# Gate of 1536 columns by Strassen units, the last 512 by token blocks, the embedding product ahead of the GLU

## The chip, the cores and the metric

The kernel runs on one core of one Trainium2 chip. The metric is the device time of one execution in microseconds; three runs of the kernel before took 1724.1, 1725.99 and 1729.99, median 1725.99. A core has five engines with a queue each: TensorE (PE, matmuls into PSUM), VectorE (DVE), ScalarE (ACT), GpSimd (POOL) and SyncE (SP, which here only issues transfers). Each works through its own instructions in order and waits for the others by semaphores. Transfers between DRAM and the on-chip memory SBUF are done by 16 DMA engines. In this kernel DVE and ACT read matmul results from PSUM; POOL and the transfers work on SBUF.

## The reference

Sequence 1024 (tokens), model width D = 2048, everything float32. Cut to what matters:

```python
hn = rmsnorm(h, norm_gain)
proj = hn @ w_in                     # 2048 x 4096: pool input | pool gate | ssm input | ssm gate
ya = pool_mixer(pool_in, w_pool, pool_scale) * silu(pool_gate)   # trailing means, windows 2/4/8/16
g  = gelu(ssm(ssm_in))               # state space, groups of 16 channels
hg = g @ w_glu                       # 1024 x 2048
yb = hg[:, :1024] * sigmoid(hg[:, 1024:]) * silu(ssm_gate)
h  = h + concat([ya, yb]) @ w_out    # 2048 x 2048
h  = h + (p @ w_ple) * sigmoid(h @ w_ple_gate)   # 256 x 2048 and 2048 x 2048: embedding and gate
out = rmsnorm(h, final_gain)
```

## The kernel before

Most data is kept transposed: channels on the 128 partitions, tokens along the rows, in two halves of HT = 512 tokens. A float32 product is made of three matmuls of a rounded type: both operands are split into a high and a low part (ACT casts the high part, DVE subtracts to get the low one), and high x high, high x low and low x high are added up in PSUM. One matmul has 128 x 128 fixed and 128 x 512 moving operands. All splits of weights (`split`, buffer `w`) and of data (`slot`, tag S, 32 buffers) are instructions of ACT and DVE that PE waits for.

The program is a list of steps of about 12 matmuls, written in order. `emit(s)` issues, for step s: the loads of weight chunks that have a free buffer (`raw`, three), the stores that are due (`store` keeps each one or more steps back), the splits of the weights of up to four steps ahead as far as six `w` buffers allow (a Strassen step takes two, so three steps), then the functions hung on the step ahead of it ("pre"), a slice of the background work (state space, pooling windows), the step's matmuls, and the functions behind it ("post"). So the order on every engine is the order of these calls, and a pre function that waits on ACT or DVE holds back the weight splits behind it. Tiles of 128 x 512 come from one rotating pool (`st`, 11 buffers): a new tile waits until the one eleven allocations back has been left by all its users, a transfer included. SP's transfers use eight completion semaphores in turn, so one waits until the eighth before it has landed.

The stages, with their place in the profile: input product (0 to 815 us) with the state-space work and the pooling windows beside it; the GLU (819 to 988), the output product (988 to 1296), and the gate with the embedding product (1296 to the end).

GLU and output product are made by `unit`: one of Strassen's seven-product schemes over quadrants. A unit takes 1024 input channels and two blocks of 256 output columns for all tokens, and has seven products (PRODS) of two steps, 12 matmuls a step, 168 in all, where a direct product has 192. The weights' sums are made on DVE (`sums`, four of 128 x 1024 a unit), the sums of the data beforehand and once for all units of a slab (`sums_load`, `sums_make`, stored in `cm_d`), and the 28 combinations of a slab are loaded and split two a step (`comb_load`, `comb_split`, tile `cb`). The products' parts are put together by a post function: `glu_post`, `o_post`. In the output product a slab n is one half of the 2048 input channels; `xt_load` brings the residual (from `xT_d`, in slab 1 from `h_d`), each part is added to it by DVE (tile `xtl`), and the sum is stored to `h_d`.

The gate runs per half h and group cg of 512 output columns in `wide_step`s: tokens on the partitions, the data as fixed operand, the weights (128 x 512) as moving one, 16 steps, then `embed`, two steps of the embedding product into other banks. `sig` takes the sigmoid, `join` multiplies by the embedding product and adds to `nat`, the token-major copy of h, which POOL's `hs_pre` (high plus low part), PE's `back` (transposes, tile `bk`) and `back_copy` make. `squares` sums squares and lets POOL multiply by the gain. In the last group (cg 3, h 1) the split weights stay (`wl`) and the work goes by blocks of 128 tokens, the last of them in two halves of 256 columns (`last_part`), so that little is left behind the last matmul.

The input product's last two blocks, 2 and 3, have their second half of tokens last (from `i_last0` to `i_last1`); then the GLU's first unit follows, then the pooling product of group 1 (`pool_mm(1)`), then the other units. POOL makes `lw` and the add in `lm` for the state space (`ss_l`) and the adds of the pooling windows (`pool_win`, tile `pf`).

## Time and profile before

| | us |
|---|---|
| median of three runs | 1725.99 |
| the profiled execution | 1725.38 |
| its span on the core | 1723.6 |
| PE busy | 1682.1 |
| DVE busy | 1108.0 |
| ACT busy | 660.3 |
| POOL busy | 282.4 |

The profile names an instruction by its line, its engine and the tiles it writes and reads, as `mm<-hn,w`: it writes a bank named mm and reads hn and w. L99 is the helper `tt` (an operation on two tensors), so its rows tell DVE's and POOL's work apart by tiles. A row of a group has the count, the busy time in all, the mean of one in ns, and the idle time of the engine ahead of it with what ended it. The chain of waits goes back from the last instruction, at each step to what released it. A row by stretches has the stretch, its length, then busy time and count of PE, PE's weight loads, DVE, ACT and POOL, PE's granted clock, the DMA engines' busy share and GB/s. A transfer row has the count, the size of one, and the median time from issue to landing.

### The profile page before, as it was taken

To read this page: it belongs to the slowest core of one execution; us is meant where nothing else is said; L and a number is where in the kernel's file an instruction comes from. 1 tells how busy PE (TensorE), PEld (TensorE's weight loads), DVE (VectorE), ACT (ScalarE), POOL (GpSimd) and SP (SyncE) were. 2 spreads that over 40 slices of the span, in tenths; PEclk is the share of its full clock that TensorE was granted. 3 is DMA by queue.
4 is the path that set the end of the run, shared out by engine and by line. 5 is a ranking of instruction groups with operands and counts; after the bars stand their busy time and mean duration, and the time that the engine had idled before them with its cause. 6 is when DMAs were issued, how large, how long until landed. Compare 5 with 4: busy or idle time off the path is not lost.

```text
span 1723.6 us, 22772 instructions
## 1 busy us (share of the span) xinstructions
PE 1682.1 (98%) x7766; PEld 1390.3 (81%) x7766; DVE 1108.0 (64%) x1992; ACT 660.3 (38%) x1379; POOL 282.4 (16%) x327
## 2 busy tenths in 40 slices
PE   8999999999999999999899999999999999999997
PEld 7788877888888888787688778888888777877786
DVE  5763688468786655555967887695574655466642
ACT  6651255352114542333533532252232433343432
POOL 0057135000000214311100000000000332023320
PEclk9999999999999999999999999999999999999999
DMA  8863434452233854677566778684454333363312
GB/s 262 245 186 80 116 126 136 148 184 76 77 105 119 244 151 117 177 213 235 193 232 207 273 268 287 226 307 146 170 179 171 117 122 108 113 220 120 113 56 98
DMA packets 283382, 289.73 MB, mean 168 GB/s; under 512 B 53993, under 2 KB 187138, under 8 KB 282370
## 3 DMA queue, kind: packets, MB, share of 16 engines
q1 hardware_dynamic: 283266, 288.28, 51.2%
q8 instruction: 61, 1.00, 0.2%
q14 instruction: 55, 0.45, 0.1%
HBM read 204.85 MB, written 83.36 MB: 167 GB/s over the span
## 4 chain that ended last, share of the span: by engine, by line
PE 50%; DVE 3%; DMA 2%; issue 2%; ACT 1%; POOL 1%; ACTq 0%; POOLq 0%; SPq 0%; DVEq 0%
PE mm L244 18%; PE mm L232 16%; PE aux L232 7%; PE mm L254 7%; PE aux L244 2%; DVE w L99 1%; PE bk L1355 1%; DVE cb L99 1%; DMA cb<-gq_d 1%; POOL nat L99 1%; DMA cb<-cm_d 1%; DMA wq<-in_w_out_dram 0%; ACT cb L406 0%; DMA sgt<-sg_d 0%; DVE wq L99 0%
## 5 line engine op out<-in xcount | busy, mean ns | idle before, releaser
L254 PE MATMUL mm<-hn,w 128*128 128x512 f32 x3072 | 724.8, 394 | 7.0 <-DVE w L99 2.7
L254 PEld LDWEIGHTS mm<-hn,w 128*128 128x128 f32 x3072 | 574.4, 189 | 127.2 <-DVE w L99 4.0
L99 DVE TENSOR_TENSOR w<-raw,w 128x256 fp32r<-128x256 f32 (+1 forms) x440 | 272.4, 632 | 277.4 <-ACT w L217 147.5
L232 PE MATMUL mm<-cb,w 128*128 128x512 f32 x1440 | 334.3, 390 | 7.5 <-DVE w L99 4.5
L244 PE MATMUL mm<-w,h 128*128 128x512 f32 x1359 | 320.0, 392 | 6.1 <-DVE w L99 6.1
L232 PEld LDWEIGHTS mm<-cb,w 128*128 128x128 f32 x1440 | 269.1, 188 | 68.0 <-DVE w L99 7.7
L244 PEld LDWEIGHTS mm<-w,h 128*128 128x128 f32 x1359 | 252.2, 188 | 60.1 <-DVE w L99 9.1
L210 ACT CAST w<-raw 128x256 fp32r<-128x256 f32 x312 | 123.1, 406 | 274.5 <-PE mm L254 218.8
L200 ACT CAST w<-wq 128x512 fp32r<-128x512 f32 x144 | 89.1, 621 | 206.0 <-PE mm L232 84.6
L217 ACT CAST w<-raw 128x512 fp32r<-128x512 f32 x128 | 79.3, 620 | 209.1 <-PE mm L244 153.2
L232 PE MATMUL aux<-cb,w 128*128 128x512 f32 x576 | 135.3, 390 | 2.4 <-DVE w L99 1.3
L99 POOL TENSOR_TENSOR hs<-h 128x512 f32<-128x512 f32 x32 | 51.7, 1639 | 490.5 <-DMA h_d<-xtl 452.8
L232 PEld LDWEIGHTS aux<-cb,w 128*128 128x128 f32 x576 | 107.9, 188 | 25.9 <-DVE w L99 2.2
L99 DVE TENSOR_TENSOR w<-wq,w 128x512 fp32r<-128x512 f32 x144 | 101.3, 703 | 16.4 <-ACT w L200 16.4
L99 DVE TENSOR_TENSOR xtl<-mm,xtl 128x512 f32<-128x512 f32 x80 | 55.1, 689 | 47.0 <-PE mm L232 46.9
L99 POOL TENSOR_TENSOR nat<-nat,fg 128x512 f32<-128x512 f32 x28 | 45.8, 1668 | 237.8 <-ACT sig L1381 210.2
L99 POOL TENSOR_TENSOR pf<-pf 128x1023 f32<-128x1023 f32 (+7 forms) x28 | 45.5, 1627 | 151.1 <-DVE pf L99 139.1
L99 POOL TENSOR_TENSOR ytm<-yt,mask 128x512 f32<-128x512 f32 x16 | 19.6, 1222 | 306.2 <-DMA yl<-L_d 178.3
L99 DVE TENSOR_TENSOR cb<-cb 128x512 fp32r<-128x512 f32 x84 | 58.0, 726 | 15.3 <-ACT cb L406 15.3
L406 ACT CAST cb<-cb 128x512 fp32r<-128x512 f32 x84 | 49.0, 619 | 24.2 <-DMA cb<-gq_d 9.6
L244 PE MATMUL aux<-w,p 128*128 128x512 f32 x192 | 44.8, 389 | 0.0
L99 DVE TENSOR_TENSOR sig<-aux,sig 128x512 f32<-128x512 f32 (+1 forms) x33 | 22.0, 668 | 31.2 <-ACT sig L1371 20.8
(209 smaller groups left out, 1573.4 us busy)
## 6 DMA issues: line engine op xcount, KB each, us to landing
raw<-in_w_in_dram SPq DMA_DIRECT2D x136, 256.0 KB, 2.9
raw<-in_w_ple_gate_dram SPq DMA_DIRECT2D x112, 256.0 KB, 3.1
wq<-in_w_out_dram SPq DMA_DIRECT2D x16, 1024.0 KB, 9.2
h_d<-xtl SPq DMA_DIRECT2D x64, 256.0 KB, 3.0
cb<-cm_d SPq DMA_DIRECT2D x48, 256.0 KB, 5.4
xT_d<-xt SPq DMA_DIRECT2D x32, 256.0 KB, 4.1
wq<-in_w_glu_dram SPq DMA_DIRECT2D x16, 512.0 KB, 7.6
xtl<-xT_d SPq DMA_DIRECT2D x32, 256.0 KB, 5.5
```

The costliest lines, as they stand in the source:

```text
L99: eng.tensor_tensor(out=o, in0=a, in1=b, op=op)
L200: act.copy(out=w[0], in_=src)
L210: act.copy(out=w[:, 0], in_=raw)
L217: act.copy(out=hi, in_=raw)
L232: pe.matmul(out=banks[key], lhsT=w[wi][:, kp], rhs=a[:, ai], start=bool(new) and n == 0, stop=n == 11, skip_group_check=True)
L244: pe.matmul(out=banks[key][:, part], lhsT=a[:, ai, cols], rhs=b[:, part], start=start and j == 0, stop=stop and j == 2)
L254: pe.matmul(out=banks[key], lhsT=w[:, wi, i], rhs=a[:, ai], start=start and i == 0 and j == 0, stop=stop and i == 1 and j == 2)
L406: act.copy(out=sl[:, 0], in_=f(sl[:, 1]))
L1355: pe.transpose(fin["b"][tb][:, (k % 4) * P:(k % 4 + 1) * P], hs[:, tb * P:(tb + 1) * P], ident)
```

## The change

1. Output product: no residual is loaded. `o_post` copies a part that comes first from PSUM with ACT, adds the second part with DVE where there is one, and adds the result to `xT_d` in DRAM by an accumulating transfer on POOL's queue. After both slabs `xT_d` holds h; `h_d` is gone.
2. The gate's columns 0 to 1535 are six more units (two slabs of input channels, three groups of 512 columns), with the sums and combinations of h (`srcs[3]`, `srcs[4]`) made as those of ya and yb. Slab 0's sums go to `ps_d`. In slab 1 they are loaded again together with the embedding product (`e_d`), and sigmoid, product and an accumulating transfer add the result to `z_d`, which three transfers of 2 MB within DRAM have filled with h.
3. Columns 1536 to 2047 are done by eight blocks of 128 tokens with the split weights kept (`wl`). Each block loads and splits its h (`h_load`, `h_split`), turns z and the last columns of h by PE (`z_turn`), takes squares and gain, joins, and scales and stores the block before (`final`).
4. The embedding product comes ahead of the GLU: 12 column blocks channel-major into `e_d`, the last 512 columns token-major into `en_d`, `pool_mm(1)` between. The GLU's first unit loads its weights as the others do, and the combinations for the GLU are spread over these steps.
5. In `ss_l` and `pool_win` the named POOL operations are DVE's.

```diff
-                tt(pool, wv, bc4(pr["L2"], g0), pw(pr["PI"], g0, 1), ALU.mult)
-                tt(pool, m, m, w, ALU.add)
+                tt(dve, wv, bc4(pr["L2"], g0), pw(pr["PI"], g0, 1), ALU.mult)
+                tt(dve, m, m, w, ALU.add)
...
-            tt(pool, dst[:, sh:], src[:, sh:], src[:, :L - sh], ALU.add)
-            pool.tensor_copy(out=dst[:, 0:sh], in_=src[:, 0:sh])
+            tt(dve, dst[:, sh:], src[:, sh:], src[:, :L - sh], ALU.add)
+            dve.tensor_copy(out=dst[:, 0:sh], in_=src[:, 0:sh])
...
+    for m in range(12):
+        if m == 8:
+            pool_mm(1)
+        block(w_ple[:, :, m * P:(m + 1) * P], [0, 1], (0, 1), p_key, ("em", m), e_post(m))
+    for h in range(2):
+        for k in range(2):
+            wide_step(chunk(w_ple[:, k, 3 * HT:], 4),
+                      [(("en", h, tb), mm, (("p", k), h), tok(tb), None, k == 0, k == 1)
+                       for tb in range(4)],
+                      post=[lambda tb=tb, h=h: en_post(h, tb) for tb in range(4)] if k else ())
...
-    for i, at in enumerate((i_last0, gu[0][1] + 9, gu[1][1] + 1, gu[2][1] + 2)):
+    for i, at in enumerate((i_glu - 6, i_glu - 1, gu[1][1] + 2, gu[2][1] + 2)):
...
+            def add(c, h, t):
+                pool.dma_start(out=pair(xT_d, 4 * cg + 2 * c + b, h), in_=t, accum_op=ALU.add)
+
+            if prod in ("11", "s2", "s3", "s4"):
+                k, c, h = {"11": ("a", 0, 0), "s2": ("a", 0, 1), "s3": ("e", 1, 1),
+                           "s4": ("a", 1, 0)}[prod]
+                t = ot[c, h, b] = st(name="ot")
+                act.copy(out=t, in_=banks[name, k, b])
+                if prod == "s4":
+                    add(c, h, ot.pop((c, h, b)))
+                return
+            k, c, h = {"12": ("f", 0, 0), "s1": ("a", 1, 1), "22": ("e", 0, 1)}[prod]
+            t = ot.pop((c, h, b))
+            tt(dve, t, banks[name, k, b], t, ALU.add)
+            add(c, h, t)
...
+    def gate_out(n, mb, h, t):
+        if n == 0:
+            store(pair(ps_d, mb, h), t)
+            return
+        act.activation(out=t, in_=t, func=AF.Sigmoid)
+        tt(dve, t, t, zt.pop(("e", mb, h)), ALU.mult)
+        pool.dma_start(out=pair(z_d, mb, h), in_=t, accum_op=ALU.add)
...
+    for n in range(2):
+        for cg in range(3):
+            u = {}
+            s0 = unit(u, ("n", n, cg), ("h", n), n_post(n, cg))
+            units.append((u, s0))
+            if n:
+                for at, c, h, key in ((0, 0, 0, "s"), (2, 0, 0, "e"), (4, 0, 1, "s"),
+                                      (6, 1, 1, "s"), (8, 1, 1, "e"), (10, 1, 0, "s"),
+                                      (11, 1, 0, "e"), (12, 0, 1, "e")):
+                    for b in range(2):
+                        steps[s0 + at + b - 2]["pre"].append(
+                            lambda mb=4 * cg + 2 * c + b, h=h, key=key: z_load(
+                                ps_d if key == "s" else e_d, mb, h, key))
+    for cg in range(3):
+        steps[units[5 + cg][1] + 8]["pre"].append(lambda cg=cg: sp.dma_start(
+            out=z_d[cg * HT:(cg + 1) * HT], in_=xT_d[cg * HT:(cg + 1) * HT]))
...
+    for j, s0, d in ((0, gu[1][1], 6), (1, i_c, 7), (3, units[6][1] - 3, 4), (4, units[8][1], 6)):
...
+    def z_turn(tb, g):
+        z = fin.pop(("z", tb, g))
+        b = aux("bk")
+        for i in range(4):
+            pe.transpose(b[:, i * P:(i + 1) * P], z[:, i * P:(i + 1) * P], ident)
+        if g == 3:
+            fin["hb", tb] = b
+            return
+        act.activation(out=z, in_=b, func=AF.Square, accum_out=sq_of(tb)[:, g:g + 1])
+        tt(dve, nat(tb)[:, g * GW:(g + 1) * GW], b, fin["fg"][g], ALU.mult)
```

PE's order at the passage from the output product to the gate, before. `mm` and `aux` are PSUM banks, `cb` a combination of yb, `w` split weights, `h` split data, `hs` the sum of its parts:

```order
L232 MATMUL mm<-cb,w 128x512 x48
L232 MATMUL aux<-cb,w 128x512 x24
L244 MATMUL mm<-w,h 128x512 x36
L1355 MATMUL bk<-ident,hs 128x128 x4
L244 MATMUL mm<-w,h 128x512 x12
L1355 MATMUL bk<-ident,hs 128x128 x4
```

And with the change, from the last gate unit to the first token block (`wl` split weights that stay, `zn` a tile of z or h):

```order
L235 MATMUL mm<-cb,w 128x512 x72
L235 MATMUL aux<-cb,w 128x512 x24
L235 MATMUL mm<-cb,w 128x512 x48
L235 MATMUL aux<-cb,w 128x512 x24
L247 MATMUL mm<-wl,h 128x512 x12
L1454 MATMUL bk<-ident,zn 128x128 x4
L247 MATMUL mm<-wl,h 128x512 x12
```

The gate's wide steps have become units of 72 + 24 + 48 + 24 = 168 matmuls, and the transposes stand in the token blocks alone.

SP's order where the GLU begins, before (`wq` weights of a unit, `cb` combinations of g, `sgt` the SSM gate, `ya_d` results of the pooling product):

```order
L182 DMA ya_d<-pgt 128x512 x2
L327 DMA wq<-in_w_glu_dram 128x4x256 x4
L182 DMA ya_d<-pgt 128x512 x2
L190 DMA raw<-in_w_in_dram 128x4x128
L401 DMA cb<-gq_d 128x512 x2
L190 DMA raw<-in_w_in_dram 128x4x128
L401 DMA cb<-gq_d 128x512 x2
```

And with the change, at the end of the embedding product (`et` its results):

```order
L185 DMA e_d<-et 128x512 x2
L333 DMA wq<-in_w_glu_dram 128x4x256 x4
L396 DMA cb<-gq_d 128x512
L185 DMA e_d<-et 128x512 x2
L396 DMA cb<-gq_d 128x512
L185 DMA e_d<-et 128x512 x2
L396 DMA cb<-gq_d 128x512
L185 DMA e_d<-et 128x512 x2
L396 DMA cb<-gq_d 128x512
L185 DMA en_d<-et 128x512 x4
L333 DMA wq<-in_w_glu_dram 128x4x256 x4
```

The weights of the first GLU unit have moved behind most of the combinations, which now come one a step between the stores of the embedding product.

SP's order in the last output unit with the change (`cq` quarters of h for sums, `cs` and `cq` to `cm_d` the sums); the copy to `z_d` stands among the combinations of h:

```order
L329 DMA wq<-in_w_ple_gate_dram 128x4x512 x2
L396 DMA cb<-xT_d 128x512 x2
L185 DMA cm_d<-cs 128x512
L185 DMA cm_d<-cq 128x512 x3
L396 DMA cb<-xT_d 128x512 x6
L396 DMA cb<-cm_d 128x512 x2
L185 DMA cm_d<-cs 128x512
L185 DMA cm_d<-cq 128x512 x3
L396 DMA cb<-cm_d 128x512 x2
L1358 DMA z_d<-xT_d 32x16384
L396 DMA cb<-cm_d 128x512 x12
```

Before, nothing of this stood here: the residual's loads and stores did, and the loads of h's first tiles.

More of the change, by code (lines that the diff above doesn't have):

```diff
@@ L1255, in hybrid_trunk @@
-    units = []
-    for n in range(2):
-        for cg in range(4):
-            u = {}
-            s0 = unit(u, ("o", n, cg), ("y", n), o_post(n, cg))
-            units.append((u, s0))
-            for at, c, h in ((0, 0, 0), (4, 0, 1), (6, 1, 1), (10, 1, 0)):
-                for b in range(2):
-                    i = max(s0 + at + b - 3, units[0][1] - 2)
-                    steps[i]["pre"].append(lambda mb=4 * cg + 2 * c + b, h=h, n=n: xt_load(
-                        h_d if n else xT_d, mb, h))
@@ new lines, in hybrid_trunk @@
+    for i in range(4):
+        steps[i_last0 - 6 + 3 * i]["pre"].append(lambda i=i: p_load(i % 2, i // 2))
+        steps[i_last0 + 1 + 3 * i]["pre"].append(lambda i=i: p_proc(i % 2, i // 2))
+    i_glu = len(steps)
+    gu = []
+    for j in range(4):
+        u = {}
+        s0 = unit(u, ("g", j), ("g", 0), glu_post(j))
+        gu.append((u, s0))
+        for b in range(2):
+            for at, h in ((1, 0), (7, 1)):
+                steps[s0 + at + b]["pre"].append(lambda mb=2 * j + b, h=h: sg_load(mb, h))
@@ new lines, in hybrid_trunk, with z_load @@
+    units = []
+    for n in range(2):
+        for cg in range(4):
+            u = {}
+            s0 = unit(u, ("o", n, cg), ("y", n), o_post(n, cg))
+            units.append((u, s0))
+    i_c = units[0][1]
+    zt = {}
+    def z_load(src, mb, h, key):
+        zt[key, mb, h] = st(name="z" + key)
+        sp.dma_start(out=zt[key, mb, h], in_=pair(src, mb, h))
+    def gate_out(n, mb, h, t):
[5 more added lines that the diff above has]
+        pool.dma_start(out=pair(z_d, mb, h), in_=t, accum_op=ALU.add)
@@ new lines, in hybrid_trunk @@
+    prs = [(kp, kp + 4) for kp in range(4)]
+    srcs = {0: ya_d, 1: yb_d, 2: gq_d, 3: xT_d[0:W], 4: xT_d[W:]}
+    for j, s0, d in ((0, gu[1][1], 6), (1, i_c, 7), (3, units[6][1] - 3, 4), (4, units[8][1], 6)):
+        for kp in range(4):
+            at = s0 + 4 + d * kp
+            steps[at]["pre"].append(lambda j=j, kp=kp: sums_load(j, srcs[j], kp, prs[kp]))
+            steps[at + 5]["pre"].append(lambda j=j, kp=kp: sums_make(j, kp))
+    slabs = {0: ("y", 0), 1: ("y", 1), 2: ("g", 0), 3: ("h", 0), 4: ("h", 1)}
@@ new lines, in hybrid_trunk @@
+    for j, s0 in ((0, gu[3][1]), (1, units[3][1]), (2, None), (3, units[7][1]),
+                  (4, units[10][1])):
+        for i, prod in enumerate(PRODS):
+            for kp in range(4):
+                n = 4 * i + kp
+                if s0 is not None:
+                    at = s0 + 2 * i + 4 + kp // 2
+                elif n < 12:
+                    at = i_last0 + 5 + n
+                else:
+                    at = i_last1 + 2 + (n - 12)
+                steps[at - 2]["pre"].append(lambda j=j, prod=prod, kp=kp: comb_load(
+                    j, srcs[j], prod, kp, prs[kp]))
+                steps[at + (j == 2)]["pre"].append(lambda j=j, prod=prod, kp=kp: comb_split(
+                    slabs[j], j, prod, kp))
@@ L1358, in back_copy, with wl_load @@
[L1358 to L1367 removed]
+    def wl_load(k):
+        fin["wl", k] = r_p.tile([P, 4, P], F32, tag="raw", name="raw").rearrange("p a c -> p (a c)")
+        sp.dma_start(out=fin["wl", k], in_=w_ple_gate[:, k, 3 * GW:])
@@ new lines, in h_split, with zn_load, en_load @@
+    def h_split(tb, g):
+        sl = fin.pop(("h", tb, g))
+        for i in range(4):
+            acts["h", tb, 4 * g + i] = sl[:, :, i * P:(i + 1) * P]
+        act.copy(out=sl[:, 0], in_=f(sl[:, 1]))
+        tt(dve, sl[:, 1], f(sl[:, 1]), f(sl[:, 0]), ALU.subtract)
+    def zn_load(tb, g):
+        fin["z", tb, g] = st(name="zn")
+        sp.dma_start(out=fin["z", tb, g].rearrange("p (k t) -> p k t", k=4),
+                     in_=rows4(xT_d if g == 3 else z_d, g, tb))
+    def en_load(tb):
+        fin["en", tb] = st(name="en")
+        sp.dma_start(out=fin["en", tb], in_=en_d[tok(tb)])
```

375 lines of the change are left out of this document (131 added, 244 removed).

## The prediction

> **What bounds the kernel now.** I read the engine table first, then the chain of waits, then busy time by stretch.
>
> ```profile
> span 1723.6 us, 22772 instructions
> PE 1682.1 (98%) x7766; PEld 1390.3 (81%) x7766; DVE 1108.0 (64%) x1992; ACT 660.3 (38%) x1379; POOL 282.4 (16%) x327
> ```
>
> PE (TensorE) is busy 98% of the span. Its busy time is modelled, so I take the rate from two undisturbed pieces of the chain (start, length, what):
>
> ```profile
> 1028.85 16.32 PE mm L232 x72
> ...
> 1314.58 27.23 PE mm L244 x120
> ```
>
> 16.32/72 and 27.23/120 are both 0.2267 us for each 512-wide matmul, in a Strassen unit (L232) and in the gate (L244) alike. So each matmul taken from PE is worth 0.227 us wherever PE does not wait. Where it does wait (columns: stretch, PE busy, PEld, DVE, ACT, POOL, clock, DMA share, GB/s):
>
> ```profile
> 400.00:600.00 200.00, 199.81 (x968) 168.43 (x967) 155.44 (x505) 65.24 (x151) 13.48 (x11) 1.00 0.42 126
> 600.00:790.00 190.00, 187.94 (x872) 156.69 (x871) 104.21 (x177) 66.95 (x132) 48.94 (x49) 1.00 0.58 170
> 790.00:815.00 25.00, 23.19 (x94) 18.44 (x93) 12.20 (x20) 8.96 (x20) 4.16 (x3) 0.93 0.79 260
> 815.00:860.00 45.00, 38.82 (x164) 29.89 (x163) 42.46 (x63) 25.84 (x49) 9.44 (x10) 1.00 0.56 195
> 940.00:1005.00 65.00, 61.25 (x262) 48.15 (x261) 54.15 (x82) 33.26 (x61) 0.00 (x0) 1.00 0.75 266
> 1005.00:1290.00 285.00, 285.00 (x1263) 235.98 (x1262) 202.91 (x298) 86.38 (x145) 1.94 (x2) 1.00 0.63 222
> 1345.00:1400.00 55.00, 54.16 (x246) 44.27 (x246) 32.24 (x39) 20.72 (x40) 13.22 (x8) 1.00 0.37 123
> 1400.00:1500.00 100.00, 98.34 (x450) 80.27 (x449) 52.62 (x61) 37.26 (x71) 25.96 (x16) 1.00 0.33 113
> 1500.00:1530.00 30.00, 28.59 (x125) 23.05 (x124) 22.27 (x31) 14.54 (x26) 13.64 (x12) 1.00 0.53 197
> 1530.00:1660.00 130.00, 127.55 (x582) 104.41 (x582) 68.58 (x81) 49.29 (x91) 31.32 (x19) 1.00 0.38 127
> ```
>
> PE idles 8.0 us before and in the first GLU unit (790 to 860), 3.75 us from the last GLU unit into the first output unit (940 to 1005), nothing in the output units, and 0.84+1.66+1.41+2.45 = 6.4 us in the gate stage (1345 to 1660). The rest (the start, the end, the state-space part) the change hardly touches.
>
> **The change, part by part.**
>
> *Less matmul.* Gate columns 0 to 1535 go from 1152 matmuls to 6 units of 7 products, 6 x 168 = 1008. The last 512 columns, the embedding (192) and the 128 transposes keep their numbers. 144 x 0.2267 = **-32.6 us**, all on PE, which sets the end.
>
> *The gate's own idles* belong to wide steps that no longer exist: **-6.4**. Their successors have the splits and sums of an output unit:
>
> ```profile
> L99 DVE TENSOR_TENSOR w<-wq,w 128x512 fp32r<-128x512 f32 x144 | 101.3, 703 | 16.4 <-ACT w L200 16.4
> L99 DVE TENSOR_TENSOR xtl<-mm,xtl 128x512 f32<-128x512 f32 x80 | 55.1, 689 | 47.0 <-PE mm L232 46.9
> L99 DVE TENSOR_TENSOR cb<-cb 128x512 fp32r<-128x512 f32 x84 | 58.0, 726 | 15.3 <-ACT cb L406 15.3
> L99 DVE TENSOR_TENSOR wq<-wq 128x1024 f32<-128x1024 f32 x24 | 29.2, 1218 | 0.0
> ```
>
> A unit lasts 168 x 0.2267 = 38.1 us. A gate unit of the second half asks DVE for 14 splits (9.8), 4 sums (4.9), 14 adds (9.6) and 8 products (5.5): 30 us, which fits. The last one also has most of the 16 splits of the last weights (11): about 41 us, over by some 3. I charge **+3** (0 to 10) where the token blocks begin, and **+1** (0 to 12) for the other units: the SP loads of old sums there reuse buffers that an accumulating transfer must first have left, three steps (8 us) earlier in the program (rival C).
>
> *Embedding product ahead of the GLU.* It puts 49 us of PE work (18 steps of 2.72) between the last input block and the GLU, and spreads the 28 loads of GLU combinations over it. What PE waited for:
>
> ```profile
> 798.97 7.40 DMA cb<-gq_d
> ...
> 809.51 3.19 DMA cb<-gq_d
> ...
> 823.54 5.36 DMA cb<-cm_d
> ```
>
> ACT stood at a combination that had not landed, with the weight casts behind it. Now 2 MB of GLU weights no longer stand ahead of these loads, but SP must move 32 stores of products, 17 combinations, 8 tiles of the pooling product and 4 wide weight loads (61 x 0.262 MB), 14 half-size loads (1.8 MB) and the weights (2.1): 19.9 MB in 49 us, 406 GB/s. The best stretch shown reaches 353:
>
> ```profile
> 1064.00:1083.00 19.00, 19.00 (x85) 15.73 (x85) 14.94 (x21) 4.36 (x7) 0.00 (x0) 1.00 0.97 353
> ...
> 1121.00:1140.00 19.00, 19.00 (x86) 15.73 (x85) 18.71 (x31) 11.87 (x21) 0.00 (x0) 1.00 0.90 309
> ```
>
> So transfers end the section 19.9/0.353 - 49 = 7 us late; loads run 8 us ahead of their cast and weights three steps ahead of PE, which covers most. Between a full cure (-8.0) and as much lost again plus the 7 (+7) I take half: **-4**. At the first output unit the order of loads stays (2 MB of weights, then combinations), but the 32 loads of the residual leave: **-2** (-3.75 to +1).
>
> *POOL's adds on DVE.* From 192 to 306 us DVE takes over 16 products and 16 adds, later 20 adds of the pooling windows:
>
> ```profile
> L99 POOL TENSOR_TENSOR lm<-lm,lw 128x512 f32<-128x512 f32 x16 | 23.1, 1442 | 32.8 <-DVE lm L99 24.8 <-issue 3.9 <-ACT lh L847 3.2
> L99 POOL TENSOR_TENSOR lw<-qb,qa 128x512 f32<-128x512 f32 x16 | 21.8, 1365 | 61.9 <-PE aux L757 33.6 <-DMA L_d<-lo 9.9 <-DVE m L99 7.4
> ...
> L99 DVE TENSOR_TENSOR w<-raw,w 128x256 fp32r<-128x256 f32 x13 | 8.5, 650 | 6.1 <-ACT w L210 6.1
> ...
> L99 DVE TENSOR_TENSOR w<-raw,w 128x256 fp32r<-128x256 f32 x9 | 3.7, 411 | 0.6 <-ACT w L210 0.6
> ```
>
> The last two rows are one DVE operation at 193 to 240 us, beside POOL's pairs, and at 285 to 306: 650 against 411 ns. DVE gains 32 x 0.7 = 22 us of work and loses perhaps half of that in such stretching; the wait of ACT on POOL goes too. Where both meet, DVE is 89% full already and PE idles 3.65 us:
>
> ```profile
> 240.00:280.00 40.00, 36.35 (x163) 29.36 (x162) 35.56 (x56) 20.61 (x38) 16.06 (x12) 0.96 0.36 120
> ```
>
> If half the gained work is shed, DVE ends near 95% there. **0** in sum (-3: the idle time goes; +8: the shed half does not come).
>
> *Sums to DRAM.* 64 + 24 accumulating transfers on POOL's queue replace, for the residual, 64 loads and 64 stores on SP. No row shows one. Bounds: a plain store, 3.0 us, and the load and store that they replace, 5.5 + 3.0:
>
> ```profile
> h_d<-xtl SPq DMA_DIRECT2D x64, 256.0 KB, 3.0
> ...
> xtl<-xT_d SPq DMA_DIRECT2D x32, 256.0 KB, 5.5
> ```
>
> I take 6, nearer the upper, since destination bytes are read too. Their readers (the gate's sums, the copies to z, the first turns) follow 5 to 16 us behind, so nothing is charged but the +1 above. Behind a late one stand SP's next loads, then DVE, then PE. The Trainium skill (DMA: Bandwidth & Descriptors, Anatomy of one DMA) fits a transfer from this queue as 2.0 us plus bytes over 436 GB/s, an estimate of 2.6 us for 256 KB; by it every such wait vanishes and the +1 is 0. No run shows it yet.
>
> *Copies to z and combinations of h* meet in the last output unit: 28 combinations (7.3 MB), weights 2.1, one copy 2.1, sums 2.1, accumulates 2.1 (4.2 if what they read counts). That is 15.7 to 17.8 MB in 38 us against 13.4 MB at 353 GB/s: 6 to 12 us late, of which 5 (load two steps ahead) plus 5 (weights ahead) are covered. **+2** (0 to 10). The Trainium skill, on the same page (DMA: Bandwidth & Descriptors, Rules for kernel authors), speaks against the change here: spreading transfers over issuing engines adds no bandwidth, all run on the same 16. If accumulates were free beside SP's, 13.6 MB would remain and this term would be 0.
>
> *Token blocks.* Four transposes hold PE for 0.36 us, 0.09 each:
>
> ```profile
> 1304.37 0.60 PE L1355 MATMUL bk<-ident,hs 128*128 128x128 f32 x4
> 1304.73 3.02 PE L244 MATMUL mm<-w,h 128*128 128x512 f32 x12
> ```
>
> There are eight blocks of 48 x 0.2267 + 16 x 0.09 = 12.3 us; each moves 3.4 MB, 281 GB/s, 2.1 of it in 512-byte rows. The row at 400 to 600 us, mostly such rows, gives 126/0.42 = 300 at full share (estimate): it just holds. **+2** (0 to 14). DVE needs 4 splits of h, 3 gain products, 2 joins and 2 scalings, 11 x 0.7 = 8 us of each 12.3, and ACT no more. The end is the same:
>
> ```profile
> 1714.17 0.52 PE L244 MATMUL mm<-w,h 128*128 128x256 f32 x3
> ```
>
> 9 us follow this last matmul in both.
>
> Sum: -32.6 - 6.4 + 3 + 1 - 4 - 2 + 0 + 2 + 2 = -37.0. The profiled execution took 1725.38 us (span 1723.6 and 1.8 around it): 1688.4. The median shown, 1725.99, is 0.6 above it: **1689 us**.
>
> **Rivals.** *B, transfers decide at three places.* For: 406 and up to 467 GB/s asked against 353. Against: 309 GB/s at 0.90 share beside 28 combinations cost PE nothing. The GLU entry loses 12 instead of 4 (+8), the last output unit 8 instead of 2 (+6), the token blocks 5 more: 1708 us. *C, the accumulates are slow* (the slower side). One landing after 8 us holds SP at the buffer it has not left; DVE waits for the next load, PE for DVE. At 20 us each of three gate units loses 12, and the turns of the first token block, planned 16 us behind, 8: 1689 + 44 - 1 = 1732. It decides above 8 us for half the gain and at 18 us for the sign. Against: load plus store are 8.5 now. *D, all entry idles go*: -8.0 and -3.75 instead of -4 and -2, another 1.5 of the 2.06 at 600 to 790, where DVE's pooling chain shortens, and 7 of the 8 charged go: 1689 - 14 = 1675.
>
> **How the numbers follow.** Forecast 0.64 (its own range 1679 to 1701), B 0.19, D 0.11, C 0.06. The range 1674 to 1712 holds the forecast, D's centre and most of B. A measurement here tells 0.3% (5.2 us), so faster means under 1720.8: the forecast, D and nearly all of B, 0.91; within 0.3%: 0.04; slower, C alone: 0.05.
>
> **What would show it.** Right: 0.2267 us still per matmul, PE busy near 1650 us, the stretch before and in the first GLU unit with 3 to 6 us idle, output and gate units nearly gapless, accumulates landing within 4 to 8 us. Wrong: ACT waiting for combinations over 5 us at a time before the GLU or in the last output unit (B), SP waiting for accumulates in gate units 4 to 6 (C), PE waiting for transposes or h in the token blocks, or DVE over 95% from 192 to 306 us with PE idle beside it.

## The result, and the profile after

The changed kernel takes **1705.9 us** (median of four runs, 1704.9 to 1707.9) against 1727.3 for the kernel before on the same chip: ratio 0.988, 95% interval 0.986 to 0.990. It is 21.3 us faster; 37 were forecast. The profiled execution has a span of 1703.3 us, 20.3 less than before, and the rest of this text works with these two executions.

The head of the page of the changed kernel, and of its list of transfers the row of the accumulates:

```profile
span 1703.3 us, 22940 instructions
PE 1655.8 (97%) x7622; PEld 1369.0 (80%) x7622; DVE 1115.7 (66%) x2148; ACT 718.2 (42%) x1511; POOL 160.2 (9%) x267
...
xT_d<-ot POOLq DMA_DIRECT2D x64, 256.0 KB, 6.4
```

PE has 144 matmuls fewer, is busy 26.3 us less and *idle 6 us more* than before (47.5 against 41.5 us). The idle time that is new is mostly in two places. PE's timeline (start, length, what, and in brackets the idle time before it with what ended it), first in the last output unit:

```profile
1301.41 8.00 PE L235 MATMUL mm<-cb,w 128*128 128x512 f32 x34 [1.22 <-DVE w L102]
...
1318.62 0.73 PE L235 MATMUL mm<-cb,w 128*128 128x512 f32 x2 [2.62 <-ACT w L203]
1320.08 12.36 PE L235 MATMUL mm<-cb,w 128*128 128x512 f32 x46 [0.73 <-DVE w L102]
1340.37 4.94 PE L235 MATMUL aux<-cb,w 128*128 128x512 f32 x12 [5.21 <-ACT w L203]
1345.15 16.50 PE L235 MATMUL mm<-cb,w 128*128 128x512 f32 x72
```

then at the first token block:

```profile
1582.87 4.89 PE L247 MATMUL mm<-wl,h 128*128 128x512 f32 x12 [5.68 <-ACT h L1430]
1591.36 1.12 PE L1454 MATMUL bk<-ident,zn 128*128 128x128 f32 x4 [3.60 <-DMA zn<-xT_d]
1592.13 5.31 PE L247 MATMUL mm<-wl,h 128*128 128x512 f32 x12
...
1597.63 3.02 PE L247 MATMUL mm<-wl,h 128*128 128x512 f32 x12
```

Behind these waits twelve matmuls take 4.94, 4.89 and 5.31 us; the next twelve, in the last row, take 3.02. So a wait costs more than its length. The windows of the changed kernel show why (stretch, PE busy, PEld, DVE, ACT, POOL, granted clock, DMA share, GB/s):

```profile
815.00:865.00 50.00, 46.20 (x192) 37.34 (x191) 25.56 (x46) 29.37 (x59) 0.00 (x0) 0.93 1.00 357
...
1255.00:1291.00 36.00, 36.00 (x161) 29.81 (x160) 21.53 (x31) 11.96 (x21) 6.42 (x8) 1.00 0.93 262
1291.00:1345.00 54.00, 43.63 (x171) 33.84 (x170) 33.43 (x50) 22.95 (x42) 6.07 (x7) 0.91 0.97 312
...
1580.00:1587.00 7.00, 4.13 (x10) 3.15 (x11) 3.28 (x5) 2.47 (x5) 0.86 (x1) 0.51 1.03 264
...
1590.00:1597.00 7.00, 5.64 (x16) 4.58 (x17) 1.99 (x3) 1.55 (x3) 0.00 (x0) 0.52 1.09 301
```

Behind these waits of PE the granted clock is one half for some microseconds, and the DMA share is at or near 1 in each stretch shown in which PE waits.

The eighteen units are the best ruler in this kernel: from the first matmul of one to the first of the next, 168 matmuls at 0.2267 us make 38.08. Twelve of the 18 take this to 0.05 us, the last output unit 53.73. The following table is worked out that way from the starts in PE's timelines; it says how much each place takes beyond its matmuls and transposes (0.2267 and 0.109 us each), and also when the third pooling product (`pool_mm(0)`, about 30 us ahead of the end of the input product) starts, since up to there little but POOL's adds differs between the kernels.

| kernel | third pooling product starts | from there to the GLU | last GLU and first output unit | last output and first gate unit | last gate unit and token blocks |
|---|---|---|---|---|---|
| before | 786.4 | 12.2 (with the first GLU unit) | 6.0 | (other program) | (other program) |
| changed | 780.2 | 7.8 | 5.6 | 15.7 | 18.1 |
| copies to z later | 778.9 | 8.5 | 5.3 | 2.8 | 17.8 |
| loads for the token blocks earlier | 780.5 | 8.6 | 5.6 | 15.6 | 6.4 |
| adds back on POOL | 787.0 | 8.1 | 5.0 | 15.8 | 16.2 |
| plain stores for accumulates | 780.1 | 8.1 | 5.9 | 8.0 | 16.9 |
| copies on POOL's queue | 781.2 | 8.3 | 5.4 | 11.5 | 17.9 |
| both moves | 779.5 | 8.1 | 5.4 | 3.6 | 6.4 |
| both moves, again | 779.3 | 9.2 | 5.4 | 2.7 | 6.4 |
| both, weights moved | 779.9 | 12.3 | 3.7 | 5.7 | 7.0 |
| both, combinations later | 781.5 | 6.5 | 2.9 | 5.5 | 7.1 |
| both, some combinations later | 779.9 | 6.9 | 3.0 | 3.0 | 7.5 |

A place that an edit doesn't touch agrees from row to row within 2 us, and mostly within 1, so each experiment can be read at its own place and not only from the total.

### The profile page after: what moved, and what is told of

It reads as the page before. It is cut to its first block, busy times and chain, and to the rows that moved or that the text cites. A ratio compares the mean times of both kernels' runs of the same rounds, so it can differ in the third digit from the quotient of the medians.

```text
span 1703.3 us, 22940 instructions
## 1 busy us (share of the span) xinstructions
PE 1655.8 (97%) x7622; PEld 1369.0 (80%) x7622; DVE 1115.7 (66%) x2148; ACT 718.2 (42%) x1511; POOL 160.2 (9%) x267
## 3 DMA queue, kind: packets, MB, share of 16 engines
q0 software_dynamic: 12672, 23.07, 8.6%
## 4 chain that ended last, share of the span: by engine, by line
PE 47%; DMA 6%; DVE 3%; issue 2%; ACT 1%; SPq 0%; ACTq 0%; POOLq 0%; POOL 0%; DVEq 0%
PE mm L235 23%; PE aux L235 9%; PE mm L257 9%; PE mm L247 5%; DMA cb<-cm_d 1%; DMA cm_d<-cq 1%; DMA raw<-in_w_ple_gate_dram 1%; PE bk L1454 1%; DVE cb L102 1%; DMA e_d<-et 1%; DMA cb<-ya_d 1%; DMA zn<-xT_d 1%; DVE w L102 1%; DVE zs L102 0%; DMA cb<-xT_d 0%
## 5 line engine op out<-in xcount | busy, mean ns | idle before, releaser
L235 PE MATMUL mm<-cb,w 128*128 128x512 f32 x2160 | 500.8, 391 | 8.6 <-ACT w L203 3.1
L235 PEld LDWEIGHTS mm<-cb,w 128*128 128x128 f32 x2160 | 405.4, 188 | 98.2 <-DVE w L102 5.1
L102 DVE TENSOR_TENSOR w<-raw,w 128x256 fp32r<-128x256 f32 (+1 forms) x328 | 141.0, 441 | 121.4 <-ACT w L213 113.3
L102 DVE TENSOR_TENSOR w<-wq,w 128x512 fp32r<-128x512 f32 x216 | 148.3, 686 | 104.0 <-ACT w L203 103.7
L235 PE MATMUL aux<-cb,w 128*128 128x512 f32 x864 | 205.5, 393 | 7.7 <-ACT w L203 7.7
L235 PEld LDWEIGHTS aux<-cb,w 128*128 128x128 f32 x864 | 163.0, 189 | 44.4 <-ACT w L203 9.3
L203 ACT CAST w<-wq 128x512 fp32r<-128x512 f32 x216 | 133.6, 620 | 134.3 <-PE mm L235 54.8
L1286 POOL DMA_DIRECT2D xT_d<-ot x64 | 55.4, 866 | 670.3 <-DVE ot L102 634.7
L247 PE MATMUL mm<-wl,h 128*128 128x512 f32 (+1 forms) x432 | 100.9, 386 | 5.7 <-ACT h L1430 5.7
L247 PEld LDWEIGHTS mm<-wl,h 128*128 128x128 f32 x432 | 75.7, 196 | 19.2 <-ACT h L1430 6.1
L499 ACT ACTIVATE gs<-mm 128x512 f32<-128x512 f32 x32 | 18.9, 598 | 58.3 <-DVE mm L102 57.0
```

The source lines that it names most:

```text
L102: eng.tensor_tensor(out=o, in0=a, in1=b, op=op)
L203: act.copy(out=w[0], in_=src)
L235: pe.matmul(out=banks[key], lhsT=w[wi][:, kp], rhs=a[:, ai], start=bool(new) and n == 0, stop=n == 11, skip_group_check=True)
L247: pe.matmul(out=banks[key][:, part], lhsT=a[:, ai, cols], rhs=b[:, part], start=start and j == 0, stop=stop and j == 2)
L499: act.activation(out=s, in_=b, func=AF.Sigmoid)
L1286: pool.dma_start(out=pair(xT_d, 4 * cg + 2 * c + b, h), in_=t, accum_op=ALU.add)
```

## The experiments

### The copies to z later

In the last output unit ACT stands at combinations of h that have not landed. The waits of ACT from 1285 to 1345 us in the changed kernel (waiting, releaser, us in total, times, longest), and two rows of SP's timeline there (start, length):

```profile
ACT cb L401 <- DMA cb<-cm_d: 11.8, 3, 8.9
ACT cb L401 <- DMA cb<-xT_d: 9.6, 3, 5.4
```

```profile
1324.87 0.48 SPq L1358 DMA_DIRECT2D z_d<-xT_d  x1
1325.45 14.89 SPq L396 DMA_DIRECT2D cb<-cm_d  x12
```

A 2 MB copy goes ahead of twelve loads of combinations, and the chain of waits of that stretch has this load as its longest piece:

```profile
1326.07 12.61 DMA cb<-cm_d
```

The edit takes the three copies out of the output units:

```diff
-    for cg in range(3):
-        steps[units[5 + cg][1] + 8]["pre"].append(lambda cg=cg: sp.dma_start(
+    for cg, at in ((0, units[8][1] + 4), (1, units[9][1] + 1), (2, units[9][1] + 8)):
+        steps[at]["pre"].append(lambda cg=cg: sp.dma_start(
```

> The three 2 MB copies of h to z are moved out of the output units 6 to 8 into the first two gate units; everything else is as changed. Theory T (the copies, which hold all 16 DMA engines for 10 us beside 28 combinations and stand in SP's queue ahead of them): the last output unit falls from 53.7 us to 38 to 43, both half-clock stretches beside it go, time 1690 to 1696 us. Rival R (28 combinations, their sums and the accumulates are too much by themselves, and SP stands on free buffers): the last output unit stays above 49 us, time 1702 or more. Half way: 1697 to 1701, both have a share.

Measured: 1692.7 us (ratio to the kernel before 0.9802, interval 0.9789 to 0.9814), 13.2 less than the changed kernel. That is theory T's time. The last output unit with the first gate unit loses 2.8 us instead of 15.7, no other place moves, and no half-clock stretch is left there. The window of that unit, and of ACT's waits from 1285 to 1345 us the row on the combinations' loads:

```profile
1291.00:1331.00 40.00, 38.33 (x167) 30.93 (x166) 33.75 (x51) 22.64 (x42) 6.93 (x8) 1.00 1.02 312
```

```profile
ACT cb L401 <- DMA cb<-cm_d: 4.9, 8, 1.4
```

ACT's longest such wait is 1.4 us, where it was 8.9. The DMA share is as full as it was and the rate the same 312 GB/s, but 12.5 MB go through in the unit's 40 us where 16.8 MB went in 54. The copy is 2.1 MB of the difference; the rest are loads that fall on the other side of a window's end, such as the last four quarters of h, which leave SP at 1288.9 us here and at 1296.7 in the changed kernel. In the gate units the copies cost PE half a microsecond.

The copy at 1324.87 us is not the whole cause. By PE's timeline of the changed kernel, 8.2 of the 15.7 us are lost up to 1332.28 us, behind waits that had ended by 1320.08, before that copy left; only 7.4 are lost behind it. The copy of the unit before left at 1269.97 us, and the weights of the last output unit left SP at 1298.6 us, where they leave at 1290.8 with the copies moved. This run moved all three copies at once, so it doesn't say how much each of them cost.

### The same copies from POOL's queue

The copy above did two things: it took bandwidth, and it stood on SP's queue, which waited for it to land, as a row of SP's waits from 1255 to 1345 us in the changed kernel shows:

```profile
SPq L396 <- DMA z_d<-xT_d: 5.0, 1, 5.0
```

This run keeps the bytes and the place in the program and takes the copies off SP's queue:

```diff
-        steps[units[5 + cg][1] + 8]["pre"].append(lambda cg=cg: sp.dma_start(
+        steps[units[5 + cg][1] + 8]["pre"].append(lambda cg=cg: pool.dma_start(
```

> The three copies to z stay at their places in the output units, but GpSimd's queue issues them instead of SP's, so that nothing on SP stands behind one. Theory O (order on SP's queue: loads and stores stand behind a copy that waits for its accumulates, and behind its completion): the last output unit falls from 53.7 to 45 us or less, time 1697 or less. Theory T (bandwidth: a copy takes all 16 DMA engines for its 10 us whoever issues it): it stays at 50 us or more, time 1702 to 1709.

Measured: 1702.4 us (0.9856, 0.9842 to 0.9869), 3.5 less. The last output unit takes 49.6 us and loses 11.5 instead of 15.7, between the two theories and close to T, which holds for most of it: of the 12.9 us that the copies cost there (15.7 - 2.8), 4.2 go with the queue and the rest stays with the bytes. The split is not a clean one, since the edit also moved the copy in time: it left 17 us earlier, at 1308 us, and the loads beside it were late in its place. The window of that unit in this run:

```profile
1293.00:1343.00 50.00, 41.23 (x171) 32.72 (x170) 35.07 (x53) 23.49 (x44) 7.49 (x9) 0.93 1.02 325
```

The Trainium skill says so beforehand (DMA: Bandwidth & Descriptors, Issuing engines are not separate DMA queues): transfers of all issuing engines share the same 16 DMA engines, and a second issuer saves only issue time. The run agrees for the larger part. The 4.2 us are not issue time, which is 0.48 us for the copy on SP: SP's wait of 5.0 us for the copy is gone here, and the copy leaves earlier.

### Plain stores in place of the accumulates

```diff
-                pool.dma_start(out=pair(xT_d, 4 * cg + 2 * c + b, h), in_=t, accum_op=ALU.add)
+                pool.dma_start(out=pair(xT_d, 4 * cg + 2 * c + b, h), in_=t)
```

> The 64 accumulating transfers of the output product become plain stores of the same tiles from the same queue, so h lacks the residual and the first slab's part: the sum in DRAM is left out. Theory A (what the accumulate reads back is DMA traffic that the last output unit lacks): landings fall from a median of 6.4 to 3 to 4 us, the last output unit shortens by 3 to 6 us, time 1699 to 1703. Rival (an accumulate costs the path no more than a store; the copies decide): time 1704.5 to 1707.

Measured: 1698.5 us (0.9830, 0.9818 to 0.9843), 7.5 less, more than either theory said. It is all in the last output unit, 15.7 to 8.0 us; no other place moves by more than 1.2. The window of that unit and the stores' row in the list of transfers, in this run:

```profile
1291.00:1338.00 47.00, 42.08 (x174) 33.94 (x173) 33.42 (x51) 22.91 (x43) 4.19 (x9) 0.93 0.97 352
...
xT_d<-ot POOLq DMA_DIRECT2D x64, 256.0 KB, 3.9
```

The group that issues them on POOL, in the changed kernel and in this run:

```profile
L1286 POOL DMA_DIRECT2D xT_d<-ot x64 | 55.4, 866 | 670.3 <-DVE ot L102 634.7
```

```profile
L1286 POOL DMA_DIRECT2D xT_d<-ot x64 | 34.8, 544 | 682.9 <-DVE ot L102 645.2
```

An accumulate lands after 6.4 us and a plain store after 3.9, and it occupies POOL for 866 instead of 544 ns. In the output units from the second to the seventh, neither costs PE anything. In the overfull one, some eight accumulates cost 7.7 us. The row of POOL's DMA queue in the list of queues (packets, MB, share of the time of 16 engines), in the changed kernel and in this run, says why:

```profile
q0 software_dynamic: 12672, 23.07, 8.6%
```

```profile
q0 software_dynamic: 8576, 23.07, 4.9%
```

The 64 accumulates count the same bytes as the 64 stores and take 64 packets more each. 8.6% of 1703.3 us less 4.9% of 1696.9 is 63 us, so an accumulate holds the 16 engines for about 1.0 us more than a store. Eight of them are 8 us, an estimate from these rows, against the 7.7 that the unit got back. The two culprits of this unit, 12.9 us for the copies and 7.7 for the accumulates, add to more than the 15.7 there are: part of the loss goes with either. Without the copies 2.8 us remain, without the accumulates 8.0.

### The loads for the token blocks earlier

At 1582.9 us PE waits for the first h, and ACT's waits from 1576 to 1600 us in the changed kernel begin with

```profile
ACT h L1430 <- DMA h<-xT_d: 10.8, 2, 7.1
```

Ahead of h ACT stands at slices of the last weights (`wl`) as each lands, since SP can have only three of them under way and stands at the fourth with the loads of h behind it. Then 1 MB of gains goes out together with h. The edit spreads the weight slices, and moves the gains and the first h ahead:

```diff
-        at = s_l + 2 + 3 * k // 4
+        at = s_l - 2 + k
-    steps[i_t[0] - 2]["pre"].append(fg_load)
+    steps[units[-2][1] + 6]["pre"].append(fg_load)
-            at = s_l + 10 + g if tb == 0 else i_t[0] + g - 2 if tb == 1 else i_t[tb - 2] + g
+            at = s_l + 6 + g if tb == 0 else i_t[0] + g - 2 if tb == 1 else i_t[tb - 2] + g
-            at = max(at + 3, i_t[tb - 1] + g) if tb else s_l + 13
+            at = max(at + 3, i_t[tb - 1] + g) if tb else s_l + 10 + g
```

> Only the loads ahead of the token blocks are moved: the 16 slices of the last gate weights one per step and from 2 steps before the last gate unit (was 4 every 3 steps from its step 2), the final gain one unit earlier, the first block's h four steps earlier with its splits one step apart. Theory Q (order: SP stands on three weight buffers, and behind it the first h and the 1 MB of gains come in one burst): the idles of 5.68 and 3.60 us and the half clock behind them go, the first token block starts within 2 us of the end of the last gate unit and the token blocks end 10 to 14 us earlier, time 1692 to 1696. Rival V (volume: the stretch is at full DMA share whatever the order): the wait only moves, time 1702 or more.

Measured: 1695.5 us (0.9813, 0.9800 to 0.9826), 10.4 less, as theory Q had it. The token blocks now begin the moment the last gate unit ends, and the place loses 6.4 us instead of 18.1. PE's timeline in this run:

```profile
1577.65 2.88 PE L247 MATMUL mm<-wl,h 128*128 128x512 f32 x12
1581.60 0.66 PE L1454 MATMUL bk<-ident,zn 128*128 128x128 f32 x4 [1.07 <-DMA zn<-xT_d]
1582.01 3.01 PE L247 MATMUL mm<-wl,h 128*128 128x512 f32 x12
```

What is left are waits of 1 us for the blocks that are turned. The same bytes in another order were enough here: unlike the last output unit, this place could spread its burst over units ahead whose share is 0.83 to 0.87.

### POOL's adds back on POOL

The start of the third pooling product is 6.2 us earlier than before, where I had forecast 0. The edit undoes the fifth part of the change alone: the six operations in `ss_l` and `pool_win` are `pool`'s again.

```diff
-                tt(dve, wv, bc4(pr["L2"], g0), pw(pr["PI"], g0, 1), ALU.mult)
-                tt(dve, m, m, w, ALU.add)
+                tt(pool, wv, bc4(pr["L2"], g0), pw(pr["PI"], g0, 1), ALU.mult)
+                tt(pool, m, m, w, ALU.add)
...
-            tt(dve, dst[:, sh:], src[:, sh:], src[:, :L - sh], ALU.add)
+            tt(pool, dst[:, sh:], src[:, sh:], src[:, :L - sh], ALU.add)
...
```

> The state-space products and adds and the pooling windows' adds go back from VectorE to GpSimd; all else as changed. Theory P (these edits alone made the stretch before the last input blocks 6 us shorter, which the forecast had at 0): time 1711 to 1713, the product of the pooling branch starts near 686 us again, PE idles 3 us or more between 240 and 280 us. Rival (the 6 us come from another edit, or are noise between two profiled executions): 1704 to 1708, and that product stays near 682.

Measured: 1715.6 us (0.9928, 0.9913 to 0.9944), 9.7 more than the changed kernel and 2.6 above theory P's 1711 to 1713. The first pooling product, which the expectation means, starts at 686.5 us instead of 681.9, and the third at 787.0 again, 6.8 later: theory P, and the gain of 6.2 us is this part's. The profiled execution, with a span of 1708.0, is the shortest of its six (1709.8 to 1719.7 us): its span is only 4.7 us above the changed kernel's, 6.8 later here and 2 given back further on. The other 5 of the 9.7 us are not in these two traces and stay open. The window from 240 to 285 us, changed and undone:

```profile
240.00:285.00 45.00, 43.17 (x197) 34.57 (x196) 42.08 (x78) 25.70 (x47) 0.00 (x0) 1.00 0.40 135
```

```profile
240.00:285.00 45.00, 40.07 (x178) 32.24 (x177) 37.86 (x62) 24.83 (x44) 18.67 (x14) 0.96 0.40 138
```

DVE is 94% full and PE has 3.1 us more of work done. From 192 to 310 us DVE has taken over two groups of 11 us and is only 8.5 us busier (100.0 against 91.5): the rest is paid back by its other work, which POOL no longer holds up. Two of these groups by shape, changed and undone:

```profile
L102 DVE TENSOR_TENSOR w<-raw,w 128x256 fp32r<-128x256 f32 x37 | 15.4, 415 | 8.3 <-ACT w L213 8.3
L102 DVE TENSOR_TENSOR lm<-lm,lw 128x512 f32<-128x512 f32 x16 | 11.1, 692 | 0.6
L102 DVE TENSOR_TENSOR lw<-qb,qa 128x512 f32<-128x512 f32 x16 | 10.9, 683 | 0.0
...
L111 DVE SCALAR_TENSOR_TENSOR ks<-same,dT,ks 64x64 f32<-64x64 f32 x15 | 4.2, 277 | 0.5
```

```profile
L102 DVE TENSOR_TENSOR w<-raw,w 128x256 fp32r<-128x256 f32 x36 | 19.7, 547 | 9.7 <-ACT w L213 9.7
...
L111 DVE SCALAR_TENSOR_TENSOR ks<-same,dT,ks 64x64 f32<-64x64 f32 x15 | 9.6, 640 | 0.5
```

And the two waits of ACT on POOL that the kernel before has from 190 to 310 us are gone:

```profile
ACT lh L847 <- POOL lm L99: 9.1, 5, 3.9
ACT lo L849 <- POOL lm L99: 8.5, 4, 3.9
```

The Trainium skill (SBUF — State Buffer, SBUF: two separate sides) explains the stretched rows by an exclusive lock on a port pair that DVE and GpSimd share: an operation of DVE with two inputs in SBUF has to wait out a GpSimd operation that reads SBUF and started first. 547 against 415 ns and 640 against 277 agree with it, as does a row with one input in PSUM (`ks<-aux,ks`, 678 ns in both); but `lm<-qb,qa`, with two inputs in SBUF, isn't stretched either (684 against 682 ns).

### Both moves

> Both moves together: the copies to z in the first two gate units and the earlier loads ahead of the token blocks. If the two places are independent the gains add: 1705.9 - 13.2 - 10.4 = 1682.3 us (1680 to 1685), no half-clock stretch between the GLU and the end, the last output unit near 40 us and the first token block within 2 us of the last gate unit. Rival (the copies now stand in the way of what the token blocks load, or one slack hides the other): 1687 or more.

Measured: 1683.3 us (0.9747, 0.9734 to 0.9761), and run once more:

> The two moves alone once more, on the same chip and beside the same runs of the kernel before, as the base of the run with later combinations: 1681 to 1685 us.

1682.6 us (0.9734, 0.9721 to 0.9748). The gains add (1682.3 by the sum). One thing was wrong in what I expected: a half-clock stretch stays at the first output unit in the first of the two runs (last section). Another stays ahead of the GLU in both.

### Three attempts at the entries

With both moves in, 8 us are still lost ahead of the GLU and 5.4 at the first output unit. First the weights, 2 MB a unit, which go out ahead of combinations:

```diff
-    for i, at in enumerate((i_glu - 6, i_glu - 1, gu[1][1] + 2, gu[2][1] + 2)):
+    for i, at in enumerate((i_last1 + 3, gu[0][1] + 2, gu[1][1] + 2, gu[2][1] + 2)):
...
-        at = (units[i - 1] if i else gu[3])[1] + 2
+        at = (units[i - 1] if i else gu[3])[1] + (5 if i in (0, 8, 11) else 2)
```

> As the two moves together, and four weight loads of 2 MB move as well: the first GLU unit's from six steps before the GLU to the start of the embedding product, the second's into the first GLU unit, and those of the first output unit and of the first and fourth gate unit three steps later, behind the first combinations. Theory T (ACT stands at a combination that landed behind 2 MB of weights): the 4.6 us in which PE waits at the end of the embedding product and the 5.3 us at the first output unit shrink to half, 1674 to 1679 us. Rival (the section is at full DMA share, so the wait only moves): 1681 or more.

Measured: 1686.2 us (0.9761, 0.9748 to 0.9775), 3 to 4 worse than both moves alone, as the rival had it. Ahead of the GLU the loss grew from 8 to 12.3 us. The wait only moved: PE now stands in the middle of the embedding product, and ACT waits up to 8.3 us for the embedding's own weights, which are 128 KB a step and now stand behind the GLU's 2 MB:

```profile
836.63 7.87 PE L257 MATMUL mm<-pd,w 128*128 128x512 f32 x24 [5.18 <-ACT et L1231]
```

```profile
ACT w L213 <- DMA raw<-in_w_ple_dram: 11.0, 4, 8.3
```

The first row is PE's timeline of this run, the second ACT's longest waits from 815 to 870 us. Then bytes instead of order: combinations nearer to their use, so that some leave the full stretch.

```diff
-                    at = s0 + 2 * i + 4 + kp // 2
+                    at = s0 + 2 * i + (7 if j in (0, 3) else 4) + kp // 2
...
-                    at = i_last1 + 2 + (n - 12)
+                    at = i_last1 + 4 + 5 * (n - 12) // 4
```

> As the two moves together, with the combinations nearer to their use: the last 16 of the GLU's 28 loads begin two steps later and come 1.25 instead of 1 step apart, so that six of them leave the embedding product for the first GLU unit; the 28 of the first slab of y and the 28 of the first slab of h come three steps later. Nothing else moves. Theory T (volume: 815 to 862 us moves all that 16 engines can, so bytes must leave it; another order of the same bytes did not help): PE's 4.3 us wait at the end of the embedding product and its slow stretch go, the first output unit's losses shrink from 4.0 to about 2 us, 1675 to 1680 us. Rival (ACT's and SP's order, or the combinations now come too late for PE): 1682 or more.

Measured: 1683.8 us (0.9748, 0.9735 to 0.9762), no gain in the total. Place by place it splits: 1.6 to 2.7 us less ahead of the GLU (6.5 against 8.1 and 9.2; PE's wait of 4.3 us went to 3.3 and not away), 2.5 less at the first output unit, and 2 to 3 us more around the first gate unit, where the combinations of h now come too late. So it was run again without those (`(4 if j else 7)` in the first line):

> As the two moves together, and of the later combinations only those of the GLU (its last 16, as before) and of the first slab of y (three steps later); those of the first slab of h stay where they were. The gains seen place by place would add to 1683.3 - 1.6 (GLU entry) - 2.5 (first output unit) = 1679 us (1677 to 1681) if the 1.9 us lost around the first gate unit came from the h combinations alone. Rival (the places trade losses with each other, or the differences are those between two executions): 1682 or more.

Measured: 1679.1 us (0.9718, 0.9704 to 0.9731), 3.5 less than both moves beside the same runs (the intervals overlap by 0.001) and 49 less than the kernel before: the sum that was expected, and the best version found. In its windows the last GLU unit and the start of the first output unit have PE busy throughout; in its timeline PE still waits 3.2 us ahead of the GLU:

```profile
981.00:1023.00 42.00, 42.00 (x187) 34.79 (x186) 34.48 (x52) 23.64 (x44) 0.00 (x0) 1.00 0.72 253
```

```profile
857.57 4.80 PE L247 MATMUL mm<-w,p 128*128 128x512 f32 x13 [3.23 <-ACT et L1237]
```

That rest was not settled. What still stands there are the 32 stores of products beside the loads; a version with fewer bytes in this stretch was not tried.

## Why the prediction was right, and where it was not

The time fell in the range (1674 to 1712) and on the side that had 0.91, but outside the forecast's own 1679 to 1701; rival B's 1708 was nearest. Two of the signs that were to show the prediction wrong came: ACT waited over 5 us for combinations in the last output unit, and PE waited for h and for transposes in the token blocks. That the time is in the range is partly luck: the gate's idles and POOL's adds brought 11.8 us more than forecast, and without them the time would have been about 1718, beyond the range. Step by step, in us (measured: differences between the two profiled executions, by the ruler above):

| step | forecast | measured |
|---|---|---|
| less matmul | -32.6 | -32.6 |
| the gate's own idles | -6.4 | -12.0 |
| POOL's adds on DVE | 0 | -6.2 |
| embedding ahead of the GLU | -4 | -4.4 |
| first output unit | -2 | -0.4 |
| copies to z and combinations of h | +2 | +15.7 |
| gate units | +1 | +3.5 |
| entry to the token blocks | +3 | +14.2 |
| token blocks | +2 | +2.0 |
| end | 0 | 0 |
| sum | -37.0 | -20.2 (the spans differ by 20.3) |

*Less matmul* was right to the digit (of the two pieces that I took the rate from, the second gives 0.2269 us, 27.23/120, and not 0.2267). Gate units 1 to 3 and 5 take 38.08 to 38.11 us, 168 times 0.2267, and nothing on the other engines stretched them. DVE, which I had at 30 of 38 us, is at 31.1 in the fourth (1459 to 1498).

*The gate's own idles* were read too small. I took PE's idle time, 6.4 us. The count says 12.0: the old stage lasted 418.5 us, from the row below to the last matmul, for 1728 matmuls of 512 columns (391.7; two of 256 count as one) and 136 transposes (14.8). The modelled busy time hid the other half; time minus counted work would have shown it. PE's timeline of the kernel before:

```profile
1296.21 8.33 PE L244 MATMUL mm<-w,h 128*128 128x512 f32 x36
```

*POOL's adds on DVE*: the rows I quoted were the right ones (650 against 411 ns, a wait of ACT on POOL) and the conclusion was too cautious. I let the waits cancel against a fuller DVE. Both happened, DVE went to 94% as forecast, but a full DVE is harmless as long as what PE waits for comes through it sooner, and two slow POOL operations (1.4 us each) had been links of that chain. That they were is read from the waits of ACT on them; the run with the adds back shows the 6 us, not which link made them. -6.2 is outside my bounds of -3 to +8.

*Copies to z and combinations of h* is the step that failed most. The size was nearly right: I had 15.7 to 17.8 MB, the larger with what accumulates read back, at 353 GB/s, 6 to 12 us late. What went through in 54 us is 16.8 MB as counted, and with the 2.1 MB that eight accumulates read back 18.9: at 353 GB/s 53.6 us, 15.5 more than the unit's 38.1. That is no proof, since a full stretch lets more through the longer it lasts; that these bytes made it late is shown by the two runs that took them out. The wrong step is the 10 us of cover that I took off because loads go out two steps and weights some steps ahead. The stretch before, 1255 to 1291 us, already runs at a share of 0.93 (row above), and the unit's weights left SP 8 us later than with the copies moved: being early is worth little when the transfers ahead are late too. The rule of the Trainium skill that I had weighed against the change here (DMA: Bandwidth & Descriptors, Rules for kernel authors: one set of 16 engines, whoever issues) spoke to the point, and the run with the copies on POOL's queue agrees for the larger part.

*Entry to the token blocks* was sized by the wrong engine. I charged 3 us of DVE for splits. DVE was not the limit: SP stood at three weight buffers in order, the first h and 1 MB of gains came in one burst behind it, PE waited 5.68 and 3.60 us, and then ran some 10 us at half clock, which cost another 5. The order that I had read could have shown it: it asks for a slice of weights every 2.04 us (four in three steps), and a buffer is held for the 5 to 6 us to its landing and then until ACT and DVE have split it, so three buffers give one every 2.2 to 3.2 us, as SP's issues from 1568 to 1579 us are spaced.

*Rival C*, accumulates so slow that SP or the gate units wait, fell: 6.4 us is within the 8 from which it was to start, near the 6 that I took, and of the gate units it could have slowed only the first of slab 1 loses 1.6 us. SP's longest wait from 1255 to 1345 us is for one of them (18.9 us), but for a plain store it is 24.1 there, so it is not their slowness. Accumulates did cost time, but as time of the DMA engines in the full unit, which I had booked under the copies ("4.2 if what they read counts": it counts). *Rival D* fell too: ahead of the GLU 7.8 us are lost and 5.6 at the first output unit.

*Rival B* had the right sentence, "transfers decide", and two of its three places. At the GLU, its first, they did not decide more than in the forecast. At the other two it had half of what came.

## What to carry to other kernels

Where a stage asks for what the DMA engines can move, compare its bytes with the rate of the same mix of transfers, and grant no cover from early loads unless the stage before has room. Bulk copies that nothing needs soon belong in a stage with a low DMA share: three moved lines were worth 13 us here, and spreading loads ahead of a stage change 10. Read losses as time minus counted work, unit by unit, and add to a wait of a few microseconds half the slow stretch behind it, where the granted clock shows one.

## What the runs showed of the hardware

**A short wait can halve TensorE's clock for about 3.4 us or twice that.** The windows above have it at a mean of 0.51 and 0.52 over 7 us, behind waits of 5.68 and 3.60 us: by estimate 6.8 us at one half. The Trainium skill (TensorE: Matmul & The Clock Gate, Part 1) gives 3413 ns as the length of a free-running window in which activity is judged, and half rate after an idle one; the lengths here agree. But the idle time need not fill a window: with both moves, 1.53 us of waiting were enough, while 1.60 us at the same place of the same kernel, run again, were not (clock 1.00 from 1002.6 to 1010 us), nor were 2.76 us in the run with all combinations later (PE's timeline and the windows, of the first and then of the last):

```profile
1001.53 2.95 PE L235 MATMUL aux<-cb,w 128*128 128x512 f32 x7 [1.53 <-ACT w L203]
...
1002.60:1006.00 3.40, 3.40 (x10) 2.66 (x9) 3.40 (x6) 3.40 (x8) 0.00 (x0) 0.50 1.05 387
```

```profile
1355.74 1.46 PE L235 MATMUL mm<-cb,w 128*128 128x512 f32 x4 [2.76 <-ACT w L203]
...
1353.00:1360.00 7.00, 4.26 (x18) 3.22 (x18) 5.24 (x9) 4.39 (x8) 0.00 (x0) 1.00 0.21 81
```

Whether that is a matter of where in the window the wait falls was not tried.

**An accumulating transfer takes longer than a store everywhere, and cost PE time only where DMA was full.** From SBUF into DRAM, 256 KB, issue to landing, in the changed kernel from 1236 to 1256 us and from 1297 to 1347 us, with the 2 MB copy of the second stretch:

```profile
xT_d<-ot POOLq DMA_DIRECT2D x6, 256.0 KB, 3.9
...
xT_d<-ot POOLq DMA_DIRECT2D x7, 256.0 KB, 7.6
...
z_d<-xT_d SPq DMA_DIRECT2D x1, 10.0
```

The plain stores of the experiment land after 2.3 us in the first stretch and 5.8 in their full unit (1293 to 1340). The 2.6 us that the prediction worked out from the Trainium skill's fit (DMA: Bandwidth & Descriptors, Anatomy of one DMA) were reached by neither of the two medians of the accumulates.

**The counted bytes leave out what an accumulate reads back.** With accumulates and with plain stores POOL's queue counts the same 23.07 MB (rows above), and from 1100 to 1220 us, where PE is busy throughout in both kernels, the rate is 193 and 192 GB/s while the DMA share is 0.75 and 0.55. So for a stretch with accumulates the share says how full it is, and the rate too little. At a share of about 1 the 16 engines moved 357 GB/s of plain loads and stores (815 to 865 us), 352 with the copies and plain stores in the last output unit, and 312 there with accumulates (1291 to 1345). Eight accumulates of 0.262 MB in 54 us are 39 GB/s, and 312 + 39 = 351: an estimate. The same sum gives 364 in the unit with the copies later and 366 with them on POOL's queue. In the stretch from 1590 to 1597 us, with the 512-byte rows of the token blocks, the rate was 301 at a share of 1.09.

**A step of a token block is 3.2 us**, not 3.07: two rows of the chain of waits,

```profile
1600.65 0.44 PE bk L1454 x4
1601.09 2.77 PE mm L247 x12
```

four transposes cost 0.44 us where I had 0.36.
